# Expert weights of a two-layer diffusion backbone in 1 MB loads of two neighbouring rows, with the slots of SBUF handed out in pairs

## Chip, cores and metric

One core of a Trainium2 chip runs the kernel. The metric is the device time of one execution in microseconds, as the median over runs.

## The reference

Two layers work on 256 latent and 256 context tokens of width 1024, all in fp32. Layer 0 mixes tokens with windowed attention, layer 1 with differential attention. A mixture of experts follows in each layer; latent and context tokens go through it in layer 0, latent ones alone in layer 1. Each token is sent to 2 of 32 experts (the best group of 8, and the two best in it):

```python
u = xblk @ w_up[e]                                      # 1024 -> 1024
y = (silu(u[:, :512]) * u[:, 512:]) @ w_down[e]         # 512 -> 1024
```

The weighted results are added to the tokens. Shift, scale and gate of every part come from `mod_w` (2 x 1024 x 6144) times SiLU of a condition vector. A final RMSNorm gives the output.

## The kernel before

The expert weights are 402.7 MB, 4 MB for one `w_up` and 2 MB for one `w_down`. Every expert is computed, for at most 64 tokens each; a branch (`tc.If`, ahead of the sixth pair) has a slow path for more. A loop runs over 16 pairs of experts per layer. For one pair, `gather` picks tokens with a one-hot matrix, `spread_tokens` turns them so that the model dimension lies on the partitions, `up` multiplies by `w_up` in 8 steps of 128 rows, `gate` makes the gated values, `turned` turns them, `down` multiplies by `w_down` in 4 steps, and `combine` adds the weighted result to the tokens. The last pair uses `down_last`, which goes by four blocks of 256 output columns, so that the end can follow block by block. TensorE's order is written out by hand in these stages, in the output projection of layer 0 and in all of layer 1; elsewhere a scheduler of the framework orders it, and it orders the other engines and the DMA queues throughout.

Most of SBUF is an arena of 43 slots of 512 KB, 128 partitions by 4 KB. `Slot()` takes one from the list `free`, `free()` puts it back at the end. Both act while the program is written, in the order of the code; on the chip, whoever writes a slot waits until its former readers are done.

All weights pass through `plan`, a list of sources in the order of use, and `Stream`. Each entry is one DMA of 512 KB on SP's queue into a slot of its own (`one`, L172 to L178). `next` issues an entry at the place in the code where its weight is used; it can run ahead on the chip as far as its slot has been out of use. Entries are issued further ahead at the start (20 of them) and before the branch (`ahead`).

Attention weights are used in fp32 halves: `split` (L510) takes the raw slot, and two more for a high part (ScalarE copy, L513) and a low part (subtraction on VectorE or GpSimd, L517), and gives the raw one back. The output projection of layer 0 has four rounds of two splits each (L1364), 24 matmuls (L1373) for each of two blocks.

Layer 1 begins in `start1` (L1413): three slots of extra row buffers (`Extra`), one for tables (`Home`), four splits ahead, eight slots `hT` for the normalized tokens, then projections for two halves of v, then k, then q. Each projection takes a split from `ws` for every two of its eight steps and calls `pre` (L1446), which keeps `ws` filled: one raw chunk, split on ScalarE and GpSimd, and then `late_mods` with 0 to 4 chunks of layer 1's `mod_w`. Each such chunk is 256 rows by 512 columns and is multiplied and added up on VectorE (L1507, L1509). There are 32 of them, by `LATE`: 4 in each of four calls, then 3 in each of four, then 1 in each of four, and none in the last eight. `late_sum` (L1476) adds the results over partitions on TensorE, four accumulators at a time.

```python
def late_mods(n):
    ...
        s, w = stream.next()
        for kk in range(2):
            ...
        s.free()
```

Of the kernel before, what the change touches and what calls it, by code (L numbers as in the profile page):

```python
# [56 lines left out]
def _hybrid_dit(ctx, tc, a, out):  # L57
# [5 lines left out]
    places = [[nc.alloc_sbuf_tensor_at(f"slot{c}{i}", [128, 1024], dt, offset=base + 4096 * i).ap()  # L63
               for c, dt in (("f", F32), ("r", F32R))] for i in range(SLOTS)]
    const = ctx.enter_context(tc.tile_pool(name="const", bufs=1))
    pool = ctx.enter_context(tc.tile_pool(name="act", bufs=1))
# [45 lines left out]
    free = list(range(SLOTS))  # L112

    class Slot:
        def __init__(self, recent=False):
            assert free, "no slot left"
            self.s = free.pop(-1 if recent else 0)

# [10 lines left out]
        def free(self):  # L129
            free.append(self.s)  # L130
            self.s = None

    class Ring:
# [29 lines left out]
    class Stream:  # L163
# [23 lines left out]
    def plan_mod(l, third, halves, k):  # L187
        w = a["mod_w"][l, k * 128:(k + 2) * 128]
        for h in halves:
            for q in range(2):  # L190
                c0 = third * 2048 + q * 1024 + h * 512
                plan.append((w[:, c0:c0 + 512].rearrange("(q p) n -> p q n", p=128), (2, 512)))

    def plan_cols(src, c0, ks=range(0, KT, 2)):
        for k in ks:
            plan.append((src[k * 128:(k + 2) * 128, c0:c0 + 512].rearrange("(q p) n -> p q n", p=128), (2, 512)))

    def plan_out(src):
        for n in range(4):
            for k in range(0, KT, 4):  # L200
                plan.append((src[k * 128:(k + 4) * 128, n * 256:(n + 1) * 256].rearrange("(q p) n -> p q n", p=128),
                             (4, 256)))

    def plan_experts(l):
        for p in range(NE // 2):
            for k in range(KT):
                for s in range(2):
                    plan.append((a["moe_w_up"][l, 2 * p + s, k * 128:(k + 1) * 128, :], (1024,)))
            for k in range(4):
                for s in range(2):  # L210
                    w = a["moe_w_down"][l, 2 * p + s]
                    if p + 1 < NE // 2:
                        plan.append((w[k * 128:(k + 1) * 128, :], (1024,)))
                    else:
                        plan.append((w[:, k * 256:(k + 1) * 256].rearrange("(q p) n -> p q n", p=128), (4, 256)))

    late_cols = [(c, h, k) for c in (3, 2, 4, 5) for h in range(2) for k in range(0, KT, 2)]

    def plan_late(n):
        for _ in range(n):  # L220
            c, h, k = late_cols.pop(0)
            c0 = c * 1024 + h * 512
            plan.append((a["mod_w"][1, k * 128:(k + 2) * 128, c0:c0 + 512].rearrange("(q p) n -> p q n", p=128),
                         (2, 512)))

    wq0, wq1 = a["win_w_qkv"][0], a["diff_w_qkv"][0]
    mod_steps = [(m // 3, m % 3, (0, 1), k) for m in range(1, 4) for k in range(0, KT, 2)]
    for d in range(4):
        for k in range(0, KT, 4):
            for q in range(2):  # L230
                c0 = q * 1024 + d * 256
                plan.append((a["mod_w"][0, k * 128:(k + 4) * 128, c0:c0 + 256].rearrange("(q p) n -> p q n", p=128),
                             (4, 256)))
        plan_cols(wq0, 1024, (2 * d,))
# [14 lines left out]
    for k in range(KT):  # L249
        plan.append((a["diff_w_o"][0, k * 128:(k + 1) * 128, :], (1024,)))  # L250
    plan_experts(1)
# [178 lines left out]

    x_slots = [Slot(recent=True) for _ in range(KT // 2)]
    xT = [x_slots[k // 2].f(2, 512)[:, k % 2] for k in range(KT)]
# [400 lines left out]
    v0s.free()  # L833

    def logit_bias(l, nr):
        ps = bank("G")
        for k in range(KT):
# [11 lines left out]
    def part(v, c0, nt, n):  # L849
        return v[:, c0:c0 + nt * n].rearrange("p (t n) -> p t n", t=nt)  # L850

    class Post:
        def __init__(self, l, nt, lb=None):
# [5 lines left out]
            if nr == 2:  # L859
# [3 lines left out]
                for h in range(2):  # L863
                    dg = row("x")
                    for k in range(4):
                        ve.tensor_scalar(dg[:, k * 128:(k + 1) * 128], ident, d[:, 4 * h + k:4 * h + k + 1], None,
                                         op0=OP.mult)
                    ps = bank("G")
                    pe.matmul(ps, ones, dg, start=True, stop=True)
                    se.activation(self.db.f()[:, h * 512:(h + 1) * 512], ps, AF.Copy)  # L870
            self.norm = Norm(self.T, 2 if nr == 2 else 4, ge, tags="s" if nr == 2 else "st")
# [14 lines left out]
        def scaled(self, k):  # L886
            l = self.l
            if k % 4 == 0:
                self.xs[k // 4] = [Slot() for _ in range(2)]
            xa = self.xs[k // 4][k % 4 // 2].f(2, 512)[:, k % 2, :self.T]  # L890
# [16 lines left out]
        def flip(self, h, tags, ks=range(4)):  # L907
            for t in range(self.nt):
# [3 lines left out]
                for k in ks:  # L912
                    pe.transpose(ps[:, k * 128:(k + 1) * 128], self.xa[4 * h + k][:, t * 128:(t + 1) * 128], ident)
                cs = slice(ks[0] * 128, (ks[-1] + 1) * 128)
                hs = slice(h * 512 + ks[0] * 128, h * 512 + (ks[-1] + 1) * 128)
                if t < 2 and len(self.tok[t]) > 1:
                    hi, lo = (v[:, hs] for v in self.tok[t])
                    se.activation(hi, ps[:, cs], AF.Copy)
                    ve.tensor_tensor(lo, ps[:, cs], hi.bitcast(F32), op=OP.subtract)
                elif self.nr == 1:  # L920
                    se.activation(self.slots[t][-1].f()[:, hs], ps[:, cs], AF.Copy, scale=self.ri[:, t:t + 1])
                elif t % 2 == 0:
                    se.activation(self.slots[t][-1].f()[:, hs], ps[:, cs], AF.Copy)
                else:
                    ve.tensor_copy(self.slots[t][-1].f()[:, hs], ps[:, cs])
            if ks[-1] == 3:
# [51 lines left out]
    def moe(l, nt, post, after, finish):  # L978
# [77 lines left out]
        for p in range(np_):  # L1056
# [17 lines left out]
            if p == IF_AT:  # L1074
# [116 lines left out]
    def spread_tokens(l, st, h):  # L1191
        ps = bank("G")
        for k in range(4):
            pe.transpose(ps[:, k * 128:(k + 1) * 128], st["x"][h][:, k * 128:(k + 1) * 128], ident)  # L1194
        o = row("t")
        ve.tensor_tensor(o.rearrange("p (k c) -> p k c", k=4), ps.rearrange("p (k c) -> p k c", k=4),  # L1196
                         mods[l][:, 3, 4 * h:4 * h + 4, 0:1].to_broadcast([128, 4, 128]), op=OP.add)
        st["xt"].append(o)

    def up(st, u, k):  # L1200
        w = [stream.next() for _ in range(2)]
        for h in range(2):
            for s in range(2):
                c0 = (k % 4) * 128 + 64 * s
                pe.matmul(u[h][64 * s:64 * s + 64, :], st["xt"][k // 4][:, c0:c0 + 64],  # L1205
                          w[s][1][:, h * 512:(h + 1) * 512], start=(k == 0), stop=(k == KT - 1))
        for s in range(2):
            w[s][0].free()

    def gate(u):  # L1210
        th, ac = row("s"), row("s")
        se.activation(th, u[0], AF.Tanh, scale=0.5)  # L1212
        ve.scalar_tensor_tensor(ac, th, 1.0, u[0], op0=OP.add, op1=OP.mult)  # L1213
        ve.scalar_tensor_tensor(ac, ac, 0.5, u[1], op0=OP.mult, op1=OP.mult)
        return ac
# [25 lines left out]
    def down(acT):  # L1241
        y = [bank("B"), bank("B")]
        for k in range(4):
            w = [stream.next() for _ in range(2)]
            for h in range(2):
                for s in range(2):
                    c0 = k * 128 + 64 * s
                    pe.matmul(y[h][64 * s:64 * s + 64, :], acT[:, c0:c0 + 64],  # L1248
                              w[s][1][:, h * 512:(h + 1) * 512], start=(k == 0), stop=(k == 3))
            for s in range(2):  # L1250
                w[s][0].free()
        return y
# [41 lines left out]
    def overflow(l, nt, key, W, ri, tok, hT):  # L1294
        T = nt * 128
        for t in range(nt):
            for h in range(2):
# [13 lines left out]
                for k in range(4):  # L1311
                    ve.tensor_scalar(hT[4 * h + k][:, t * 128:(t + 1) * 128], ps[:, k * 128:(k + 1) * 128],
                                     mods[l][:, 3, 4 * h + k, 0:1], None, op0=OP.add)
        Wov = row("p", (128, nt, NE))
# [5 lines left out]
        with tc.For_i(0, NE, 1) as i:  # L1320
# [12 lines left out]
            ve.tensor_copy(wrow[:, :T], ps[:, :T])  # L1333
            wu = a["moe_w_up"][l, bass.ds(i, 1)].rearrange("o (k p) n -> p (o k) n", p=128)
            wd = a["moe_w_down"][l, bass.ds(i, 1)].rearrange("o (k p) n -> p (o k) n", p=128)
# [178 lines left out]
    def move_x(after):  # L1514
        slots = [Slot() for _ in range(2)]
        with tc.issue_after(after.ins):
# [270 lines left out]
```

## Time and profile before

| | us |
|---|---|
| median of three runs (1555.31 to 1561.44) | 1558.62 |
| profiled execution, its own time | 1559.65 |
| its span, first to last instruction | 1557.9 |
| TensorE busy | 1459.4 (94%) |
| VectorE busy | 692.2 (44%) |
| ScalarE busy | 385.2 (25%) |
| GpSimd busy | 186.2 (12%) |

The mean DMA rate is 312 GB/s over 485.67 MB. Busy shares are means over stages with different limits: layer 0's attention ends near 214 us and its output projection near 280, layer 0's experts run to about 815 us, layer 1's attention to about 1052, its experts to the end. DMA time is the time in which a packet was under way on an engine, so it can exceed the stretch by a little.

### The profile page before, as it was taken

Reading aid. Unit: us, or ns where it says so; the run is one execution under the profiler, and the core shown is the slowest. Engines: PE = TensorE matmul, PEld = TensorE weight load, DVE = VectorE, ACT = ScalarE, POOL = GpSimd, SP = SyncE. Lnnn points to the kernel's source line nnn. Section 1 sums busy time; section 2 is a strip of 40 time slices with the busy share of each in tenths; the row PEclk is TensorE's granted clock in tenths of the full one; section 3 lists DMA queues with packets and bytes.
Section 4 is the critical chain, followed back from the end, with each engine's and each line's share of the span. In section 5 each row is a group of like instructions: output and inputs, shape, how many; then the busy total and the mean of one; then the engine's idle time right before and its main releaser. Section 6 shows DMA issues by size and latency. Waiting matters only on the chain. (4 is left out here: it accounts for less than half of the span.)

```text
span 1557.9 us, 20210 instructions
## 1 busy us (share of the span) xinstructions
PE 1459.4 (94%) x7407; PEld 802.0 (51%) x7407; DVE 692.2 (44%) x1617; ACT 385.2 (25%) x823; POOL 186.2 (12%) x147
## 2 busy tenths in 40 slices
PE   6998999799999999999997889798999899999997
PEld 4765567444444454445445578684434343443444
DVE  3348862533333343334348976863223232332333
ACT  4426652211100111001123236552111110110112
POOL 2314541000000000000014364100000000000000
PEclk9999999799999999999997999998999999999999
DMA  9777225799989999999963842477999999999992
GB/s 329 245 230 250 82 96 194 281 373 399 390 348 393 399 398 386 402 399 399 381 210 95 287 168 81 167 272 279 388 409 409 408 409 409 409 409 409 409 396 73
DMA packets 169696, 485.67 MB, mean 312 GB/s; under 512 B 20826, under 2 KB 41587, under 8 KB 169587
## 3 DMA queue, kind: packets, MB, share of 16 engines
q1 hardware_dynamic: 169088, 483.66, 81.9%
q8 instruction: 63, 1.03, 0.3%
q10 hardware_dynamic: 498, 0.60, 0.1%
q14 instruction: 47, 0.38, 0.1%
HBM read 483.16 MB, written 1.05 MB: 311 GB/s over the span
## 5 line engine op out<-in xcount | busy, mean ns | idle before, releaser
L1205 PE MATMUL ps<-slotf,row 128*64 128x512 f32 x2048 | 450.8, 595 | 2.1 <-DVE row L1196 2.1
L1205 PEld LDWEIGHTS ps<-slotf,row 128*64 128x64 f32 x2048 | 145.6, 137 | 291.1 <-issue 275.3
L1248 PE MATMUL ps<-slotf,row 128*64 128x512 f32 x960 | 212.6, 595 | 0.0
L542 PE MATMUL ps<-slotr,slotr 128*128 128x512 f32 x768 | 193.6, 405 | 9.5 <-DVE slotf L1410 4.2
L505 DVE SCALAR_TENSOR_TENSOR slotf<-ps,mod,slotf 128x256 f32<-128x256 f32 x408 | 167.3, 476 | 62.4 <-PE ps L1287 29.7
L542 PEld LDWEIGHTS ps<-slotr,slotr 128*128 128x128 f32 x768 | 145.1, 194 | 48.2 <-DVE slotf L1410 5.0
L1248 PEld LDWEIGHTS ps<-slotf,row 128*64 128x64 f32 x960 | 66.2, 137 | 124.9 <-issue 118.1
L1213 DVE SCALAR_TENSOR_TENSOR row<-row,ps 128x512 f32<-128x512 f32 x30 | 20.6, 688 | 234.4 <-ACT row L1212 234.4
L1212 ACT ACTIVATE row<-ps 128x512 f32<-128x512 f32 x30 | 17.9, 597 | 427.8 <-PE ps L1205 388.4
L1274 DVE SCALAR_TENSOR_TENSOR row<-ps,ty,row 128x512 fp32r<-128x512 f32 x60 | 45.1, 751 | 176.4 <-ACT row L1273 173.2
L1273 ACT ACTIVATE row<-ps,ty 128x512 fp32r<-128x512 f32 x60 | 41.3, 688 | 262.9 <-PE ps L1248 262.6
L1287 PE MATMUL ps<-row,row 128*128 128x512 f32 (+1 forms) x512 | 104.5, 349 | 1.1 <-DVE slotf L505 1.0
L1287 PEld LDWEIGHTS ps<-row,row 128*128 128x128 f32 x512 | 77.3, 189 | 36.6 <-ACT row L1212 21.1
L517 POOL TENSOR_TENSOR slotr<-slotf,slotr 128x1024 fp32r<-128x1024 f32 x32 | 81.0, 2543 | 90.0 <-ACT slotr L513 62.0
L1196 DVE TENSOR_TENSOR row<-ps,mod 128x512 f32<-128x512 f32 x64 | 42.7, 687 | 102.4 <-PE ps L1194 101.7
L477 POOL TENSOR_TENSOR row<-row,row 128x512 f32<-128x512 f32 (+1 forms) x13 | 15.0, 1157 | 576.0 <-PE ps L1287 519.9
L1148 PE MATMUL ps<-slotf,row 128*128 128x512 f32 x128 | 65.3, 634 | 6.9 <-PEq L1081 4.7
L1148 PE MATMUL ps<-slotr,row 128*128 128x512 f32 x256 | 70.6, 420 | 0.0
L513 ACT ACTIVATE slotr<-slotf 128x1024 fp32r<-128x1024 f32 x44 | 46.0, 1056 | 49.3 <-DMA slotf<-in_diff_w_qkv 22.9
L1148 PEld LDWEIGHTS ps<-slotr,row 128*128 128x128 f32 x256 | 48.1, 198 | 10.0 <-issue 0.8
L1509 DVE SCALAR_TENSOR_TENSOR row<-slotf,keep,row 128x512 f32<-128x512 f32 x42 | 50.6, 1222 | 1.1
L1373 PE MATMUL ps<-slotr,slotr 128*128 128x512 f32 x192 | 47.6, 399 | 0.0
(311 smaller groups left out, 1552.2 us busy)
## 6 DMA issues: line engine op xcount, KB each, us to landing
slotf<-in_moe_w_up SPq DMA_DIRECT2D x512, 512.0 KB, 9.5
slotf<-in_moe_w_down SPq DMA_DIRECT2D x256, 512.0 KB, 10.1
slotf<-in_mod_w SPq DMA_DIRECT2D x96, 512.0 KB, 6.0
slotf<-in_diff_w_qkv SPq DMA_DIRECT2D x24, 512.0 KB, 4.4
slotf<-in_win_w_qkv SPq DMA_DIRECT2D x12, 512.0 KB, 5.1
slotf<-in_win_w_o SPq DMA_DIRECT2D x8, 512.0 KB, 4.1
slotf<-in_diff_w_o SPq DMA_DIRECT2D x8, 512.0 KB, 4.4
slotf<-in_x SPq DMA_DIRECT2D x2, 512.0 KB, 4.0
```

Source lines behind the costliest of these rows:

```text
L505: ve.scalar_tensor_tensor(xT[k][:, sl], ps[:, sl], g[:, k, r:r + 1], xT[k][:, sl], op0=OP.mult, op1=OP.add)
L513: se.activation(hv, v, AF.Copy)
L517: (eng or (ge if split_i[0] % 3 == 0 else ve)).tensor_tensor(lv, v, hv.bitcast(F32), op=OP.subtract)
L542: pe.matmul(ps[t], h[:, x, ts], w[y][:, kk, :], start=(k + kk == 0 and n == 0), stop=(k + kk == KT - 1 and n == 2))
L1148: pe.matmul(g, P[:, t, :] if len(tok[t]) > 1 else P[:, t, :].bitcast(F32), v[:, hs], start=(t == 0 and i == 0), stop=(t == nt - 1 and i == ...
L1196: ve.tensor_tensor(o.rearrange("p (k c) -> p k c", k=4), ps.rearrange("p (k c) -> p k c", k=4), mods[l][:, 3, 4 * h:4 * h + 4, 0:1].to_bro ...
L1205: pe.matmul(u[h][64 * s:64 * s + 64, :], st["xt"][k // 4][:, c0:c0 + 64], w[s][1][:, h * 512:(h + 1) * 512], start=(k == 0), stop=(k == KT ...
L1248: pe.matmul(y[h][64 * s:64 * s + 64, :], acT[:, c0:c0 + 64], w[s][1][:, h * 512:(h + 1) * 512], start=(k == 0), stop=(k == 3))
L1274: ve.scalar_tensor_tensor(yl, y[h], wsl, yh.bitcast(F32), op0=OP.mult, op1=OP.subtract)
L1287: pe.matmul(out, part[:, c * 128:(c + 1) * 128], st["PT"][:, :T], start=(i == 0), stop=(i == 1))
L1373: pe.matmul(ps, w[x][:, k % 4, ms], oT0[k][1][:, y, :], start=(k == 0 and i == 0), stop=(k == KT - 1 and i == 2))
L1509: ve.scalar_tensor_tensor(acc, w[:, kk, :], keep[:, k + kk:k + kk + 1], acc, op0=OP.mult, op1=OP.add)
```

## The change

Expert weights come as 1 MB DMAs into two neighbouring slots at once (`Wide`). A partition gets two neighbouring rows of the weight, 8 KB in one piece, where it had one row of 4 KB. Row 8p + k of `w_up` then lies on partition p and is used in step k, so the tokens' 1024 columns are dealt out in that order (`deal`, `dealt` at the evacuations) and the shift that is added to them is turned likewise (`turned_shift`, new, called in `logit_bias`). Row 4p + k of `w_down` asks the same of the gated values (`gate`). The last pair's `w_down` keeps its 512 KB loads.

Slots 2i and 2i + 1 are partners; slot 42 has none. `Wide` takes the pair that has been whole for longest. `Slot()` takes the first slot of the list whose partner is not in the list, and the first of the list if there is none. `buddies` takes a whole pair for two single slots: `x_slots`, the gathered tokens' slots, the scaled copies, and `move_x` use it. All other slots, those of `split`, `hT`, `Extra` and of all loads of 512 KB among them, use `Slot()`.

```diff
+    def whole_pairs():
+        at = {i: n for n, i in enumerate(free)}
+        found = [(max(at[i], at[i + 1]), i) for i in range(0, SLOTS - 1, 2) if i in at and i + 1 in at]
+        return [i for _, i in sorted(found)]
+
     class Slot:
-        def __init__(self, recent=False):
-            assert free, "no slot left"
-            self.s = free.pop(-1 if recent else 0)
+        def __init__(self, recent=False, at=None):
+            if at is None:
+                assert free, "no slot left"
+                order = free[::-1] if recent else free
+                at = next((i for i in order if i ^ 1 not in free), order[0])
+            free.remove(at)
+            self.s = at
...
+    class Wide:
+        def __init__(self):
+            self.at = whole_pairs()[0]
+            free.remove(self.at)
+            free.remove(self.at + 1)
...
         def one(self):
-            src, shape = plan[self.pos]
+            src, shape, wide = plan[self.pos]
             self.pos += 1
-            s = Slot()
+            s = Wide() if wide else Slot()
             v = s.f(*shape)
-            nc.sync.dma_start(v, src)
+            nc.sync.dma_start(wide_places[s.at // 2] if wide else v, src)
...
     def plan_experts(l):
         for p in range(NE // 2):
-            for k in range(KT):
+            for j in range(KT // 2):
                 for s in range(2):
-                    plan.append((a["moe_w_up"][l, 2 * p + s, k * 128:(k + 1) * 128, :], (1024,)))
...
+                    w = a["moe_w_up"][l, 2 * p + s].rearrange("(p k) n -> p (k n)", k=KT)
+                    plan.append((w[:, j * 2048:(j + 1) * 2048], (2, 1024), True))
+            if p + 1 < NE // 2:
+                for j in range(2):
+                    for s in range(2):
+                        w = a["moe_w_down"][l, 2 * p + s].rearrange("(p k) n -> p (k n)", k=4)
+                        plan.append((w[:, j * 2048:(j + 1) * 2048], (2, 1024), True))
...
+    def turned_shift(l):
...
+        pe.transpose(ps[0:8, 0:128], mods[l][:, 3, :, 0], ident)
+        ve.tensor_copy(row8[0:8], ps[0:8, 0:128])
...
+        pe.matmul(ps[:, 0:128], each, row8[0:8], start=True, stop=True)
...
+    def dealt(v, k0, n):
+        return v.rearrange("t (b m) -> t b m", b=8)[:, :, 16 * k0:16 * (k0 + n)]
+
+    def deal(v):
+        return v.rearrange("t (m b) -> t b m", b=8)
...
-            self.slots = [[Slot() for _ in range(1 if t in WHOLE[l] else 2)] for t in range(nt)]
+            if WHOLE[l]:
+                self.slots = [[s] for s in buddies()]
+            else:
+                self.slots = [list(buddies()) for t in range(nt)]
...
-                    se.activation(self.slots[t][-1].f()[:, hs], ps[:, cs], AF.Copy, scale=self.ri[:, t:t + 1])
+                    se.activation(raw, src, AF.Copy, scale=self.ri[:, t:t + 1])
...
-                stream.ahead(len(free) - 1)
+                stream.ahead(len(stream.ready) + len(whole_pairs()))
...
     def up(st, u, k):
-        w = [stream.next() for _ in range(2)]
+        if k % 2 == 0:
+            st["w_up"] = [stream.next() for _ in range(2)]
+        w = st["w_up"]
...
-        ve.scalar_tensor_tensor(ac, ac, 0.5, u[1], op0=OP.mult, op1=OP.mult)
+        ve.scalar_tensor_tensor(ac.rearrange("s (k p) -> s p k", k=4), th.rearrange("s (p k) -> s p k", k=4), 0.5,
+                                u[1].rearrange("s (p k) -> s p k", k=4), op0=OP.mult, op1=OP.mult)
```

## Rows read from the trace of the kernel before

**Rows 1.** Busy time (and instructions) of each engine by stretch, clock, DMA.
```profile
core 0: us, PE busy (x) PEld busy (x) DVE busy (x) ACT busy (x) POOL busy (x), PEclk, DMA share, GB/s
500.00:700.00 200.00, 198.28 (x960) 94.58 (x958) 76.83 (x171) 22.55 (x36) 0.00 (x0) 1.00 1.01 397
842.00:916.00 74.00, 66.51 (x281) 51.60 (x280) 72.31 (x74) 22.41 (x32) 36.13 (x13) 0.98 0.73 256
1300.00:1500.00 200.00, 196.24 (x942) 83.11 (x942) 58.31 (x122) 22.76 (x41) 0.00 (x0) 1.00 1.03 409
```
**Rows 2.** TensorE in order of time (start, length): two neighbouring pairs per layer.
```profile
362.26 7.04 PE L1205 MATMUL ps<-slotf,row 128*64 128x512 f32 x32
...
394.03 7.04 PE L1205 MATMUL ps<-slotf,row 128*64 128x512 f32 x32
...
1299.80 1.88 PE L1148 MATMUL ps<-slotf,row 128*128 128x512 f32 x4
...
1328.99 1.88 PE L1148 MATMUL ps<-slotf,row 128*128 128x512 f32 x4
```
**Rows 3.** All of TensorE's waits, 1100 to 1500 us: total, times, longest.
```profile
PE ps L1194 <- DVE row L1152: 5.8, 13, 0.4
PE ps L1148 <- PEq L1081: 4.7, 1, 4.7
```
**Rows 4.** Lines L1509, L513, L517: min/median/max ns, first and last start.
```profile
L1509 DVE SCALAR_TENSOR_TENSOR row<-slotf,keep,row x42: 739/752/2901, 842.6 to 913.5; 128x512 f32<-128x512 f32 x42
...
L513 ACT ACTIVATE slotr<-slotf x44: 1040/1060/1067, 16.8 to 955.7; 128x1024 fp32r<-128x1024 f32 x44
...
  DMA slotf<-in_diff_w_qkv: 22.9, 12
...
L517 POOL TENSOR_TENSOR slotr<-slotf,slotr x32: 2335/2396/3820, 18.0 to 956.9; 128x1024 fp32r<-128x1024 f32 x32
...
L517 DVE TENSOR_TENSOR slotr<-slotf,slotr x12: 1212/1224/1943, 48.0 to 240.4; 128x1024 fp32r<-128x1024 f32 x12
```
**Rows 5.** Line L921, and who waited for line L840 (us, times).
```profile
L921 ACT ACTIVATE slotf<-ps,ri x4: 680/688/697, 1058.8 to 1060.5; 128x512 f32<-128x512 f32 x4
...
  PEld ps L844: 1.4, 2
  PE ps L844: 0.9, 1
```
**Rows 6.** DMA issues (KB each, median us to landing): 800 to 842 us; whole span.
```profile
slotf<-in_mod_w SPq DMA_DIRECT2D x4, 512.0 KB, 4.1
slotf<-in_diff_w_qkv SPq DMA_DIRECT2D x2, 512.0 KB, 3.6
...
slotf<-in_win_w_o SPq DMA_DIRECT2D x8, 512.0 KB, 4.1
```
**Rows 7.** TensorE in order of time: output projection, first projection, second `late_sum`.
```profile
241.76 5.75 PE L1373 MATMUL ps<-slotr,slotr 128*128 128x512 f32 x24
...
832.16 24.72 PE L542 MATMUL ps<-slotr,slotr 128*128 128x512 f32 x96 [1.66 <-ACT slotr L1439]
...
936.27 1.07 PE L1476 MATMUL ps<-row,ones 128*32 128x512 f32 x8
```
**Rows 8.** SP's queue in order of time, before the second expert stage.
```profile
1015.05 0.33 SPq L177 DMA_DIRECT2D slotf<-in_moe_w_down  x1
1017.40 5.45 SPq L177 DMA_DIRECT2D slotf<-in_moe_w_up  x3
```
**Rows 9.** TensorE in order of time: first and last `down_last` of each layer.
```profile
801.30 3.67 PE L1260 MATMUL ps<-slotf,row 128*64 128x256 f32 x32 [1.28 <-ACT row L1230]
...
809.03 1.95 PE L1260 MATMUL ps<-slotf,row 128*64 128x256 f32 x16
...
1535.10 3.67 PE L1260 MATMUL ps<-slotf,row 128*64 128x256 f32 x32 [1.24 <-ACT row L1230]
...
1543.15 1.95 PE L1260 MATMUL ps<-slotf,row 128*64 128x256 f32 x16
```

More of the change, by code (lines that the diff above doesn't have):

```diff
@@ L64, in _hybrid_dit @@
                for c, dt in (("f", F32), ("r", F32R))] for i in range(SLOTS)]
+    wide_places = [nc.alloc_sbuf_tensor_at(f"slotw{i}", [128, 2048], F32, offset=base + 8192 * i).ap()
+                   for i in range(SLOTS // 2)]
     const = ctx.enter_context(tc.tile_pool(name="const", bufs=1))
@@ L131, in free, with buddies, f @@
             self.s = None
+    def buddies():
+        at = whole_pairs()
+        if not at:
+            return Slot(), Slot()
+        return Slot(at=at[0]), Slot(at=at[0] + 1)
+    class Wide:
[3 more added lines that the diff above has]
+            free.remove(self.at + 1)
+        def f(self, *shape):
+            return wide_places[self.at // 2].rearrange("p (a b) -> p a b", a=shape[0])
+        def free(self):
+            free.extend((self.at, self.at + 1))
     class Ring:
@@ L191, in plan_mod @@
                 c0 = third * 2048 + q * 1024 + h * 512
[L192 removed]
+                plan.append((w[:, c0:c0 + 512].rearrange("(q p) n -> p q n", p=128), (2, 512), False))
     def plan_cols(src, c0, ks=range(0, KT, 2)):
         for k in ks:
[L196 removed]
+            plan.append((src[k * 128:(k + 2) * 128, c0:c0 + 512].rearrange("(q p) n -> p q n", p=128), (2, 512), False))
     def plan_out(src):
@@ L249, in _hybrid_dit @@
     for k in range(KT):
-        plan.append((a["diff_w_o"][0, k * 128:(k + 1) * 128, :], (1024,)))
+        plan.append((a["diff_w_o"][0, k * 128:(k + 1) * 128, :], (1024,), False))
     plan_experts(1)
@@ L429, in mod_run @@
                 done()
-    x_slots = [Slot(recent=True) for _ in range(KT // 2)]
+    x_slots = [s for _ in range(KT // 4) for s in buddies()]
     xT = [x_slots[k // 2].f(2, 512)[:, k % 2] for k in range(KT)]
@@ L833, in _hybrid_dit @@
     v0s.free()
+    moe_shift = {}
+    def turned_shift(l):
+        work = row("x")
+        mod16 = homes[l].v[:, 964:980]
+        ve.tensor_reduce(mod16, ident.rearrange("p (k a) -> p a k", a=16), axis=AX.X, op=OP.add)
+        row8, t = work[:, 0:128], work[:, 128:256].rearrange("p (b a) -> p b a", b=8)
+        ps = bank("G")
+        pe.transpose(ps[0:8, 0:128], mods[l][:, 3, :, 0], ident)
+        ve.tensor_copy(row8[0:8], ps[0:8, 0:128])
+        ps = bank("G")
+        each = work[0:8, 256:384]
+        ve.tensor_copy(each.rearrange("j (k a) -> j k a", k=8), ident[0:8, 0:8].unsqueeze(2).to_broadcast([8, 8, 16]))
+        pe.matmul(ps[:, 0:128], each, row8[0:8], start=True, stop=True)
+        ve.tensor_tensor(t, ps[:, 0:128].rearrange("p (a b) -> p b a", b=8), mod16[:, None, :].to_broadcast([128, 8, 16]),
+                         op=OP.mult)
+        moe_shift[l] = const.tile([128, KT], F32, name=f"shift{l}", tag="shift")
+        ve.tensor_reduce(moe_shift[l], t, axis=AX.X, op=OP.add)
     def logit_bias(l, nr):
+        turned_shift(l)
         ps = bank("G")
@@ L888, in scaled @@
             if k % 4 == 0:
-                self.xs[k // 4] = [Slot() for _ in range(2)]
+                self.xs[k // 4] = buddies()
             xa = self.xs[k // 4][k % 4 // 2].f(2, 512)[:, k % 2, :self.T]
@@ L1205, in up @@
                 pe.matmul(u[h][64 * s:64 * s + 64, :], st["xt"][k // 4][:, c0:c0 + 64],
-                          w[s][1][:, h * 512:(h + 1) * 512], start=(k == 0), stop=(k == KT - 1))
-        for s in range(2):
-            w[s][0].free()
+                          w[s][1][:, k % 2, h * 512:(h + 1) * 512], start=(k == 0), stop=(k == KT - 1))
+        if k % 2:
+            for s in range(2):
+                w[s][0].free()
     def gate(u):
@@ L1243, in down @@
         for k in range(4):
-            w = [stream.next() for _ in range(2)]
+            if k % 2 == 0:
+                w = [stream.next() for _ in range(2)]
             for h in range(2):
@@ L1248, in down @@
                     pe.matmul(y[h][64 * s:64 * s + 64, :], acT[:, c0:c0 + 64],
-                              w[s][1][:, h * 512:(h + 1) * 512], start=(k == 0), stop=(k == 3))
-            for s in range(2):
-                w[s][0].free()
+                              w[s][1][:, k % 2, h * 512:(h + 1) * 512], start=(k == 0), stop=(k == 3))
+            if k % 2:
+                for s in range(2):
+                    w[s][0].free()
         return y
@@ L1514, in move_x @@
     def move_x(after):
-        slots = [Slot() for _ in range(2)]
+        slots = buddies()
         with tc.issue_after(after.ins):
```

44 lines of the change are left out of this document (22 added, 22 removed).

## The prediction

> **What bounds the kernel now.** I read the table of stages first. In both expert stages TensorE is busy 98 to 99% of the time while the DMA engines also look full: 397 GB/s in the first layer, 409 GB/s in the second [rows 1]. Two full resources cannot both set the pace, so the next view is TensorE's order of time. One pair of experts takes 394.03 − 362.26 = 31.77 us in layer 0 and 1328.99 − 1299.80 = 29.19 us in layer 1 [rows 2]. Then its waits: in 400 us of layer 1 it waits 5.8 us for a VectorE copy, 4.7 us for the branch, and never for a weight [rows 3]. So TensorE sets the pace and the loads run ahead of it. At 409 GB/s one pair (12.58 MB) takes 30.76 us to load, longer than 29.19: layer 1 lives on weights fetched earlier, and loses 1.6 us of that lead per pair.
>
> The reader is then to see where loads do matter: outside the expert stages. From 842 to 916 us VectorE is busy 72.31 of 74 us [rows 1], because it adds up the 32 late chunks of `mod_w` (`late_mods`), two operations of 0.75 us for each [rows 4]. The chunks are there in time because each lands in another of some 20 free slots (counted through the code): the list is a queue, and a slot is used again only after all others.
>
> **The change, part by part.** *DMAs.* In the expert stages each layer's 384 issues become about 190, of 1 MB. Nothing waits for them now, so faster pieces are worth 0 there. What hides the loads is the lead; were it gone at the start of layer 1, 16 pairs × (30.76 − 29.19) = 25 us would show. Pairs come whole later than single slots in the attention ahead, so I take 3 of 0 to 25. Against this stands a page of the Trainium skill, "DMA: Bandwidth & Descriptors", section "Rules for kernel authors": use at least 1 MiB per DMA for the best bandwidth. By it the stage would shorten; by [rows 3] there is no wait that it could remove.
>
> *Matmuls* stay the same in number and shape. *Shuffled columns:* the gate's write and some twenty evacuations of token columns get strides. No strided one is in the rows; layer 1's four plain ones take 0.69 us each [rows 5], and the router's VectorE chain runs meanwhile. Between 0 and double, 4 × 0.69 = 2.8 us a layer, I take 1 in all. *`turned_shift`* adds two TensorE operations and some six on VectorE per layer, with one hand-over from TensorE to VectorE and back. The nearest such hand-over, `logit_bias`'s copy, made TensorE wait 0.9 us and its weight load 1.4 us over two layers [rows 5]; 0 to 5, taken as 2.
>
> *The free list.* This is the part I price highest. `Slot()` no longer takes the oldest slot. It takes the oldest whose partner is taken, a loose half; only without one does it break the oldest whole pair. Slot 42 has no partner and is always loose. With exactly one loose half, a stream of single-slot loads gets that same slot again and again: each DMA must wait until the reader of the chunk before is done. I followed the list by hand through the code.
>
> Layer 1's start. After the last expert pair all is whole but 42. `Extra` takes 42 and a pair A, A'. `Home` takes B. Four splits take B', C, C' / D, D', E / E', F, F' / G, G', H (raw, high, low). As raw slots are freed, hT's eight take H', B', D, I, I', E', G and J; J' is left loose. The projection's first two chunks give back the pair C, C' and the halves D' and E. Now `pre` is called for the first time: raw takes J', high D', low E, and J' is free again and the only loose half. All four late chunks take J'. The second call does the same (raw J', a whole pair for high and low, four chunks in J'). Then `v1s` takes J', G', H and breaks a pair, which leaves L'. From there all ten further calls that have late chunks put raw and late chunks into L': when D' and E come back, the next high and low take them again.
>
> The price of one link: a chunk lands 3.6 us after a lone issue (4.1 with four together) [rows 6], VectorE then reads it in 2 × 0.75 us [rows 4], and hand-overs take some 0.3: 5.4 us. A call's raw chunk costs 3.6 + ScalarE's 1.06 + GpSimd's 2.40 [rows 4] + 0.3 = 7.4 us. The Trainium skill bears on this link: the same page, in "Anatomy of one DMA", fits 2.0 us plus bytes over 436 GB/s, an estimate of 3.2 us for 512 KB, and its rules say to issue early and wait late, which one slot forbids. With 3.2 for 3.6 the 32 chunks would cost 13 us less; the rows' 3.6 is used.
>
> J' starts when the second chunk's matmuls end: the four chunks take 24.72 us from 832.16 [rows 7], so at 844.5. Its split's 3.5, four links (21.6), 7.4 and four links bring it to 898.6. L' carries 10 × 7.4 + 24 × 5.4 = 204 us. If it runs beside J' from 845 on, the sums are ready at 1049; if SP's queue, which is in order, keeps it behind J', at 1103. SP's order is not the plan's: of an expert's loads, `w_down` go out among `w_up` [rows 8], so a load whose slot is free overtakes. That row is nearer to the first case; I take 1060. Who waits: the matmuls of the second `late_sum` stand in TensorE's fixed order. They now run at 936.27 [rows 7], 22 us after VectorE's last late operation (913.5 + 0.75) [rows 4]. Add 5 us for the query chunks that come ahead of them: 1065 − 936 = **129 us later**, ends 115 and 172.
>
> *Tails.* In each layer the last pair's four steps of `down_last` load two single slots each, and 42 is again the only loose half: step c + 1's first DMA waits for step c's matmuls. Such a load lands in 4.1 us (`win_w_o`, the same shape) [rows 6], with 0.4 of hand-over and 1.95 of matmuls [rows 9]: 6.45 a step, 3 × 6.45 + 1.95 = 21.3 us. Now the four take 810.98 − 801.30 = 9.7 and 1545.10 − 1535.10 = 10.0 us [rows 9]. Cost 11.6 + 11.3 = **23 us**. Behind the first tail's DMAs on SP wait layer 1's tables and first `diff_w_qkv` chunks; the norm ahead of 832 covers them. Without that cover 4 us more.
>
> *Layer 0's output projection.* The loose halves are 11, 14 and 41 (partners hold `oT0`). Of the two splits in each of four rounds both take raw 11. The second's DMA waits for the first's subtraction: 4.1 + 1.06 + 1.22 (VectorE) to 2.40 (GpSimd) = 6.4 to 7.6 us [rows 4, 6], against the first half of the block's 24 matmuls, 2.9 us [rows 7]: about 4 a round, **16 us**, ends 0 (splits run ahead) and 30. *Layer 0's queries:* every second chunk's high half takes the previous chunk's low slot, four times 2.3 to 3.5 us, but TensorE's order is free there: 6, ends 0 and 26 (with 4.1 for the modulation load behind each).
>
> Sum: 129 + 23 + 16 + 6 + 3 + 2 + 1 = 180 us, on the profiled execution's 1559.65 us (its span is 1557.9; the median of the runs is 1558.62, 1 us less): **1740 us**. With all low ends it is 1559.65 + 115 + 23 = 1698; with all high ends 172 + 27 + 30 + 26 + 25 + 5 + 6 = 291 more, 1850.
>
> **Rivals.**
> *Enough halves go round (not slower).* Before, 32 chunks take 74 us, 2.3 us each. If three or more loose halves went round in layer 1, a link would cost 5.4 / 3 = 1.8 us, under 2.3, and the tails' loads would also be early: from three halves on nothing is lost and the time is 1559.65 + 3 + 2 + 1 = 1566, or 1563 with the lead whole, within the bound below. For it: some 20 slots are free at that time. Against it: they are whole pairs, and the hand count gives one. Chance 7%.
> *Larger pieces shorten the stage.* TensorE's waits for weights would be its gain, and they are 0 in [rows 3]. What is left are the loads behind the expert weights: ScalarE waited 22.9 us in all for `diff_w_qkv` [rows 4]. If sooner expert loads halved that and TensorE gained all of it, with no chain, the time were 1559.65 − 11 = 1549. Chance 3%.
> *Only part of the chain is on the path.* If a second half came loose before the second projection, the 204 us of L' would halve: sums at 845 + 102 = 947 to 899 + 102 = 1001, with the 5 us 16 to 70 us late; with the tails' 23 that gives 1599 to 1653. Against it: D' and E come back only to be taken by the next call. Chance 8%.
> *Layer 1's lead is lost as well* and SP keeps the order: 1850 and over. Chance 6%.
> The forecast, one slot for each chain, has 76%.
>
> **Numbers.** Predicted 1740. The forecast's case runs from 1698 to 1850, its bounds, and holds 76%; taking in the upper half of the partial case, 1625 to 1850 holds 8 in 10. What a measurement of this kernel can tell from no change is 0.5%, 7.8 us. Faster: 4%, the larger-pieces case and a little of the first. Same: 6%, the rest of the first. Slower: 90%.
>
> **What would show it.** After 845 us: VectorE idle before `late_mods`' operations for `mod_w` loads, 4 us each, its busy share there falling from 98% to under half; SP waiting for VectorE or GpSimd before each load; the second `late_sum` 100 to 170 us later than the end of layer 0 would put it. In the tails TensorE idle 4 us before each step for a `w_down` load. In the output projection three or four gaps of some 4 us. The pairs' 31.77 and 29.19 us unchanged, with no waits for weights. Wrong would be the prediction if the late chunks land in different slots (VectorE stays full), if a link is well under 5 us, or if the expert stages' periods move.

## The result, and the profile after

The changed kernel takes **1773.27 us** (median of four runs, 1773.09 to 1779.74) against 1559.33 (1555.31 to 1561.44) for the kernel before on the same chip: a ratio of 1.139, 95% interval 1.135 to 1.142. It is slower, as forecast; 1740 was 33 us short, and the time lies in the range of 1625 to 1850. The profiled execution has a span of 1771.7 us where before had 1557.9, so 213.8 us are to be found. Six points in TensorE's order of time place them:

| start or end on TensorE (us) | before | after | later in this stretch | forecast |
|---|---|---|---|---|
| first `up` of layer 0 | 299.61 | 322.82 | 23.2 | 22 (queries 6, output projection 16) |
| end of the last `up` of layer 0 | 797.52 | 824.88 | 4.2 | 0 (1 in all for strides) |
| second `late_sum` | 936.27 | 1128.53 | 164.9 | 129, and 11.6 for the tail ahead of it |
| first `up` of layer 1 | 1069.85 | 1267.05 | 4.9 | 2 (`turned_shift`) |
| end of the last `up` of layer 1 | 1531.32 | 1726.89 | -1.6 | 3 (lead) |
| end of the span | 1557.9 | 1771.7 | 18.2 | 11.3 (tail) |

In the third stretch 15.7 us lie before the sums that open layer 1's norm, which start at 815.49 before and 858.53 after; 149.2 lie behind them.

The page's 40 slices show the hole at once. A slice is 44 us; the digits of TensorE, VectorE and the granted clock fall together in slices 20 to 26, from about 840 to 1150 us, and the DMA engines are less than half busy there, so it is not bandwidth that is short:
```profile
PE   6999987899999999998633533788899989999996
...
DVE  3247743333333334343532221587332323232322
...
PEclk9999999899999999999676865899999999999995
DMA  9567036699899999994143323144899999999951
GB/s 338 172 214 274 2 126 234 267 401 400 332 399 401 380 401 396 385 400 132 40 142 95 107 83 107 48 179 151 338 391 422 400 419 421 421 421 422 420 224 60
```
The table of stages gives the sizes. Before, VectorE was busy 98% of the stretch with the late chunks [rows 1]. Now it is at 22.19 and 29.68 of 100 us there, and the second expert stage is unharmed:
```profile
core 0: us, PE busy (x) PEld busy (x) DVE busy (x) ACT busy (x) POOL busy (x), PEclk, DMA share, GB/s
...
930.00:1030.00 100.00, 43.39 (x147) 31.53 (x148) 22.19 (x32) 10.47 (x17) 14.26 (x6) 0.69 0.34 100
1030.00:1130.00 100.00, 42.06 (x125) 28.58 (x123) 29.68 (x40) 15.32 (x19) 27.36 (x13) 0.65 0.31 94
...
1290.00:1500.00 210.00, 201.84 (x965) 85.98 (x965) 62.18 (x126) 23.33 (x42) 0.00 (x0) 0.99 0.99 410
```
VectorE in order of time shows the chain link by link (start, length, and in brackets the idle time before and what ended it; L1577 and L1579 are `late_mods`):
```profile
929.04 1.54 DVE L1579 SCALAR_TENSOR_TENSOR row<-slotf,keep,row 128x512 f32<-128x512 f32 x2 [3.77 <-DMA slotf<-in_mod_w]
934.34 1.54 DVE L1579 SCALAR_TENSOR_TENSOR row<-slotf,keep,row 128x512 f32<-128x512 f32 x2 [3.77 <-DMA slotf<-in_mod_w]
939.64 1.54 DVE L1579 SCALAR_TENSOR_TENSOR row<-slotf,keep,row 128x512 f32<-128x512 f32 x2 [3.75 <-DMA slotf<-in_mod_w]
...
952.04 0.49 DVE L1577 TENSOR_SCALAR slotf<-slotf,keep 128x512 f32<-128x512 f32 x1 [10.27 <-DMA slotf<-in_mod_w]
```
From one late chunk to the next it is 5.30 us: 1.54 of work and 3.77 in which VectorE waits for a load that was only issued once VectorE had finished with the half (issued at 930.61, the work that began at 929.04 having ended at 930.58). From 939.64 to 952.04 it is 12.4, a raw chunk and a late one. SP's waits in the same stretch (860 to 1130; total, times, longest) name what the loads wait for: the landing of the load before, and its readers, a splitting subtraction on GpSimd (L551) and the late operations:
```profile
SPq L206 <- POOL slotr L551: 100.5, 14, 41.4
SPq L206 <- DMA slotf<-in_mod_w: 61.2, 25, 4.2
SPq L206 <- DVE row L1579: 33.4, 21, 3.7
```
And TensorE's waits (820 to 1130) show who waits at the end: the projection (L576) for split chunks, `late_sum` (L1546) for the last accumulator, and `down_last` (L1330) for its loads:
```profile
PE ps L576 <- ACT slotr L547: 66.8, 7, 16.2
PE ps L576 <- DVE slotf L1480: 38.4, 2, 36.9
PE ps L1546 <- DVE slotf L1579: 17.1, 1, 17.1
PE ps L576 <- POOL slotr L551: 12.0, 7, 2.3
PE ps L1330 <- DMA slotf<-in_moe_w_down: 10.1, 3, 4.5
```

### The profile page after: what moved, and what is told of

The parts are those of the page before. It is cut to its first block, busy times and chain, and to the rows that moved or that the text cites. A ratio compares the mean times of both kernels' runs of the same rounds, so it can differ in the third digit from the quotient of the medians.

```text
span 1771.7 us, 19500 instructions
## 1 busy us (share of the span) xinstructions
PE 1508.5 (85%) x7413; PEld 826.1 (47%) x7413; DVE 686.2 (39%) x1627; ACT 386.5 (22%) x823; POOL 179.3 (10%) x147
## 5 line engine op out<-in xcount | busy, mean ns | idle before, releaser
L1271 PE MATMUL ps<-slotw,row 128*64 128x512 f32 x2048 | 449.2, 593 | 2.1 <-DVE row L1260 2.1
L576 PE MATMUL ps<-slotr,slotr 128*128 128x512 f32 x768 | 218.8, 438 | 129.0 <-ACT slotr L547 67.2
L1271 PEld LDWEIGHTS ps<-slotw,row 128*64 128x64 f32 x2048 | 144.9, 137 | 290.2 <-issue 281.8
L576 PEld LDWEIGHTS ps<-slotr,slotr 128*128 128x128 f32 x768 | 157.7, 212 | 181.5 <-ACT slotr L547 71.9
L1317 PE MATMUL ps<-slotw,row 128*64 128x512 f32 x960 | 212.6, 595 | 0.0
L1317 PEld LDWEIGHTS ps<-slotw,row 128*64 128x64 f32 x960 | 66.1, 137 | 125.0 <-issue 125.0
L551 POOL TENSOR_TENSOR slotr<-slotf,slotr 128x1024 fp32r<-128x1024 f32 x32 | 75.9, 2378 | 266.0 <-ACT slotr L547 256.2
L1260 DVE TENSOR_TENSOR row<-ps,shift 128x512 f32<-128x512 f32 x64 | 42.7, 686 | 101.3 <-PE ps L1258 100.5
L1579 DVE SCALAR_TENSOR_TENSOR row<-slotf,keep,row 128x512 f32<-128x512 f32 x42 | 36.9, 877 | 92.3 <-DMA slotf<-in_mod_w 91.5
L1443 PE MATMUL ps<-slotr,slotr 128*128 128x512 f32 x192 | 50.9, 413 | 8.0 <-ACT slotr L547 3.8
```

The source lines that it names most:

```text
L551: (eng or (ge if split_i[0] % 3 == 0 else ve)).tensor_tensor(lv, v, hv.bitcast(F32), op=OP.subtract)
L576: pe.matmul(ps[t], h[:, x, ts], w[y][:, kk, :], start=(k + kk == 0 and n == 0), stop=(k + kk == KT - 1 and n == 2))
L1317: pe.matmul(y[h][64 * s:64 * s + 64, :], acT[:, c0:c0 + 64], w[s][1][:, k % 2, h * 512:(h + 1) * 512], start=(k == 0), stop=(k == 3))
L1443: pe.matmul(ps, w[x][:, k % 4, ms], oT0[k][1][:, y, :], start=(k == 0 and i == 0), stop=(k == KT - 1 and i == 2))
```

## The experiments

Two theories stood against each other. *The rule*: a lone free half is taken again and again, so a load waits for the reader of the load before it; each of the lead, the chain and the tails is a place where that happens. *The loads*: 1 MB transfers, or their need of whole pairs, cost the time, and the half only names who waits. The kernels start from the changed one, e5 and e6 from e1.

**e1, no preference for lone halves.**
```diff
-                at = next((i for i in order if i ^ 1 not in free), order[0])
+                at = order[0]
```


> The changed kernel, but Slot() always takes the slot that has been free longest, as before the change; the 1 MB loads, their pairs of slots, the column order and turned_shift stay. Theory (a lone free half is taken again and again, so that a load waits for the use of the load before it): the 213.8 us by which the profiled span grew go, apart from what the other parts cost, which the two traces put at 30 gates x 0.39 us = 12 and about 2 for turned_shift: 1573 us (1560 to 1585). Rival (the 1 MB loads or their need of whole pairs cost the time, and the rule only names who waits): still above 1700.

Measured: 1567.35 us, 1.0046 of before (1.0032 to 1.0060). One line gives back 206 of 214 us with every 1 MB load still in place. In layer 1's attention VectorE waits for no late chunk any more, and the second `late_sum` comes 140.3 us behind the end of layer 0's last `up` (138.8 before, 303.7 after). The rival is excluded. That `late_sum` in TensorE's order of time, first in the changed kernel and then in e1:
```profile
1128.53 1.94 PE L1546 MATMUL ps<-row,ones 128*32 128x512 f32 x8
...
942.94 1.06 PE L1546 MATMUL ps<-row,ones 128*32 128x512 f32 x8
```

**e2, 1 MB as two loads of 512 KB.**
```diff
-            nc.sync.dma_start(wide_places[s.at // 2] if wide else v, src)
+            if wide:
+                for i in range(2):
+                    nc.sync.dma_start(wide_places[s.at // 2][:, i * 1024:(i + 1) * 1024], src[:, i * 1024:(i + 1) * 1024])
+            else:
+                nc.sync.dma_start(v, src)
```


> The changed kernel with its slot rule, but each 1 MB load is issued as two loads of 512 KB (pieces of 4 KB) into the same pair of slots. Theory (the rule, not the size of the loads): 1773 us within 10, with the same idle stretch of TensorE from 860 to 1130. Rival (the size of the loads sets the time): the time moves by more than 40, down towards 1559 if large loads are what hurts, up if they hide part of the loss.

Measured: 1773.40 us, 1.1375 (1.1352 to 1.1398), the time of the changed kernel. Layer 1's pairs take 459.92 us from the first `up` to the end of the last, against 459.84 with 1 MB loads. So the size of the loads, the part that gives the change its name, moves nothing that stands out of the spread of these runs (1766 to 1777). The Trainium skill ("DMA: Bandwidth & Descriptors", "Rules for kernel authors") asks for 1 MiB or more per DMA for the best bandwidth. The page's slices of layer 1's experts do show a higher rate, 421 GB/s in the changed kernel against 409 in e2, but no TensorE wait that it could shorten.

**e3, layer 1's raw and late chunks take the oldest slot.** A flag around `stream.next()` in `late_mods` and around the split in `pre`:
```diff
-                at = next((i for i in order if i ^ 1 not in free), order[0])
+                at = order[0] if oldest[0] else next((i for i in order if i ^ 1 not in free), order[0])
...
+                oldest[0] = True
                 with tc.issue_after(h_made[0].ins):
                     s = split(*stream.next(), (2, 512), ge)
+                oldest[0] = False
...
+            oldest[0] = True
...
             s, w = stream.next()
+            oldest[0] = False
```


> The changed kernel, but the loads and splits that pre issues in layer 1's attention and the chunks of late_mods take the slot free longest; every other Slot() keeps the new rule. Theory (each term stands alone): the 149 us between the end of layer 0's experts and the last late_sum go, the rest stays: 1773 - 149 = 1624 (1610 to 1645). Rival 1 (VectorE's or ScalarE's order in that stage, not the slot, is what it waits for): above 1700. Rival 2 (the load order is given back later, in a next wait of the same stage): 1650 to 1700.

Measured: 1626.03 us, 1.0418 (1.0401 to 1.0436): 147 us come back, both rivals fall.

**e4, the tails' loads take the oldest slot**: the same flag for loads of `moe_w_down`.

> The changed kernel, but the down weights of the last pair of each layer (the eight 512 KB loads of down_last) take the slots free longest; every other Slot() keeps the new rule. Theory: the two tails, 15.7 and 18.2 us later in the trace of after, come back: 1773 - 34 = 1739 (1733 to 1750). Rival (the tails are late for the lower granted clock or for the order of the queue, and the half only names the wait): 1760 to 1775.

Measured: 1743.49 us, 1.1169 (1.1148 to 1.1189): 30 us. The steps of `down_last` show more than the sum. In the changed kernel the last tail reads (TensorE in order of time)
```profile
1730.69 1.95 PE L1330 MATMUL ps<-slotf,row 128*64 128x256 f32 x16 [1.25 <-DVE slotf L539]
1736.23 3.68 PE L1330 MATMUL ps<-slotf,row 128*64 128x256 f32 x16 [3.60 <-DMA slotf<-in_moe_w_down]
...
1743.53 3.68 PE L1330 MATMUL ps<-slotf,row 128*64 128x256 f32 x16 [2.46 <-DMA slotf<-in_moe_w_down]
...
1750.97 3.68 PE L1330 MATMUL ps<-slotf,row 128*64 128x256 f32 x16 [0.26 <-DMA slotf<-in_moe_w_down]
```
and in e4
```profile
1719.48 3.67 PE L1333 MATMUL ps<-slotf,row 128*64 128x256 f32 x32 [1.25 <-DVE slotf L542]
1723.75 1.95 PE L1333 MATMUL ps<-slotf,row 128*64 128x256 f32 x16
1727.53 1.95 PE L1333 MATMUL ps<-slotf,row 128*64 128x256 f32 x16
```
The three waits for loads are 6.3 us in all. The same 16 matmuls take 3.68 us instead of 1.95 behind them; the table of stages puts the granted clock there at 0.50, the 1.2 GHz level, and it stays there up to the end of the span. Before, the matmuls of this stretch ran at 1.00:
```profile
1690.00:1727.00 37.00, 36.46 (x175) 14.67 (x172) 8.74 (x18) 3.99 (x8) 0.00 (x0) 1.00 0.49 189
1727.00:1736.00 9.00, 4.38 (x36) 3.46 (x36) 4.81 (x13) 1.13 (x3) 0.00 (x0) 0.97 0.18 58
1736.00:1752.00 16.00, 13.05 (x58) 8.66 (x60) 2.63 (x6) 4.43 (x10) 0.00 (x0) 0.50 0.21 66
```
So in this execution waits of 6.3 us cost 18.2. The clock's part is not the same in every execution. In the profiled one of e2, with the same rule for slots and the same loads in the tail, the waits are 8.0 us, and the tail is only 11 us longer than before (37.6 against 26.6 from the end of the last `up`), since the clock came back before the last step:
```profile
1735.75 3.24 PE L1334 MATMUL ps<-slotf,row 128*64 128x256 f32 x16 [3.47 <-DMA slotf<-in_moe_w_down]
...
1742.55 3.26 PE L1334 MATMUL ps<-slotf,row 128*64 128x256 f32 x16 [2.89 <-DMA slotf<-in_moe_w_down]
...
1749.35 1.95 PE L1334 MATMUL ps<-slotf,row 128*64 128x256 f32 x16 [1.64 <-DMA slotf<-in_moe_w_down]
```
Over the traces of e2, e3, e8, e9 and e10, which all keep this tail, it costs 11 to 18 us.

**e8, the lead takes the oldest slot**: the flag is set from the start to the first expert load.

> The changed kernel, but up to the first expert load (layer 0's modulation, queries, attention and output projection) Slot() takes the slot free longest; from there on the new rule. Theory (the 23 us by which layer 0's experts start late are that stage's own loose halves): 1773 - 23 = 1750 (1745 to 1757). Rival (turned_shift and the strided token copies make the start late): 1765 to 1775.

Measured: 1748.63 us, 1.1219 (1.1198 to 1.1240); the first `up` is at 298.77. The lead is the rule's, too. With e3 and e4 the three pieces give back 147 + 30 + 25 = 202 of the 206 us of e1: the terms add up.

**e9 and e10, one of the two streams alone.** e9 sets the flag in `late_mods` only, e10 in `pre` only.

> The changed kernel, but only the chunks of late_mods take the slot free longest; the raw chunks and their splits in layer 1's attention keep the new rule, and most raw chunks then follow one another in one half. Theory (the stage is long because raw and late chunks take turns in one half, four late links of 5.3 and a raw one of 7.4 for each chunk of the projection; a raw chain by itself has a link of 7.4 against 6.2 us of TensorE's own work for a chunk, 24.72 / 4): 16 chunks x 1.2 = 19 above the 1626 of e3: 1645 (1630 to 1660). Rival 1 (the raw chunks hold the larger part): above 1690. Rival 2 (the late chunks alone): 1626 within 5.

> The changed kernel, but only the raw chunks that pre loads in layer 1's attention and their splits take the slot free longest; the late chunks keep the new rule, and find three or four lone halves in rotation, since whole pairs are now opened. Theory (one half in rotation is what costs, whoever waits in it): as with three halves in e7, where this stage was 27 longer than in e1: 1626 + 27 = 1653 (1635 to 1670). Rival (the late chunks alone make the chain of 5.3 a link): above 1720.

Measured: 1640.52 (1.0520, 1.0502 to 1.0537) and 1630.24 us (1.0452, 1.0433 to 1.0471). Freeing either stream is nearly as good as freeing both (1626.03), but the two runs do not say the same. Followed through the code, e9 leaves ten raw chunks in a row in one half: a raw chain by itself costs about 14 us. e10 leaves no chain at all: the raw chunks and their splits open whole pairs, the 32 late chunks fall into 18 slots, and a slot is taken again by the third load after it at the soonest, mostly later. Its forecast of three or four halves was wrong, which fits a time 5 us below its range. So what a chain of late chunks alone would cost was not tried; as an estimate, 32 links of 5.30 are 170 us, where all 32 chunks took 74 before [rows 1]. e9 also isolates the raw link. ScalarE's splits (L548) follow each other in one half:
```profile
927.79 1.06 ACT L548 ACTIVATE slotr<-slotf 128x1024 fp32r<-128x1024 f32 x1 [8.24 <-DMA slotf<-in_diff_w_qkv]
935.20 1.06 ACT L548 ACTIVATE slotr<-slotf 128x1024 fp32r<-128x1024 f32 x1 [5.87 <-DMA slotf<-in_diff_w_qkv]
942.76 1.06 ACT L548 ACTIVATE slotr<-slotf 128x1024 fp32r<-128x1024 f32 x1 [3.08 <-DMA slotf<-in_diff_w_qkv]
950.30 1.06 ACT L548 ACTIVATE slotr<-slotf 128x1024 fp32r<-128x1024 f32 x1 [6.48 <-DMA slotf<-in_diff_w_qkv]
```
935.20 - 927.79 = 7.4 us, then 7.6 and 7.5; but one link of 7.5 per chunk is close to the 24.72 / 4 = 6.2 us [rows 7] that TensorE needs for it, and so almost hidden.

**e7, three halves go round.**
```diff
-                at = next((i for i in order if i ^ 1 not in free), order[0])
+                loose = [i for i in order if i ^ 1 not in free]
+                at = loose[0] if len(loose) >= 3 else order[0]
```


> The changed kernel, but Slot() prefers a lone free half only while at least three are free, and takes the slot free longest otherwise; in layer 1's attention the raw and the late chunks then go round three halves in place of one. Theory (a chunk waits for the use of the chunk that had its half before, 5.3 us a link with one half): with three halves a third of that, 1.8 us a link, which the stage's own work nearly hides: 1570 to 1590. Rival (any preference for lone halves costs: 149 us divided by three stays, beside the lead of 23): about 1640.

Measured: 1611.87 us, 1.0329 (1.0313 to 1.0345), between both: a miss for the theory's number. Against e1 the first `up` is 11.6 us later, the second `late_sum` another 27.4 and layer 1's first `up` another 5.9. VectorE's waits (850 to 1000) name the loads again:
```profile
DVE row L1580 <- DMA slotf<-in_mod_w: 20.3, 11, 5.0
...
DVE row L1578 <- DMA slotf<-in_mod_w: 7.5, 3, 3.1
DVE slotf L1578 <- DMA slotf<-in_mod_w: 6.3, 2, 3.7
```
The estimate of 1.8 us a link took the three halves for the late chunks alone. Followed through the code, the three do go round, but the raw chunks take their turn in them as well: (32 x 5.3 + 12 x 7.4) / 3 = 86 us where the stretch took 74 before [rows 1], which makes 12 of the 27 us, as an estimate. SP waits 39.5 us for the late operations and 36.6 for GpSimd's subtraction in this stretch; what the rest of the 27 us is made of was not tried.

**e5 and e6, the gate's strided write.** What is left in e1 is mostly in layer 0's pairs, 4.9 us longer than before. e5 writes the gated values in plain order and so leaves out their turn to the order of the `w_down` rows; e6 puts it back by letting the transposes of `turned` read every fourth column. (The second part of the diff is e6's alone.)
```diff
-        ve.scalar_tensor_tensor(ac.rearrange("s (k p) -> s p k", k=4), th.rearrange("s (p k) -> s p k", k=4), 0.5,
-                                u[1].rearrange("s (p k) -> s p k", k=4), op0=OP.mult, op1=OP.mult)
+        ve.scalar_tensor_tensor(ac, th, 0.5, u[1], op0=OP.mult, op1=OP.mult)
...
-            pe.transpose(ps[:, k * 128:(k + 1) * 128], ac[:, k * 128:(k + 1) * 128], ident)
+            pe.transpose(ps[:, k * 128:(k + 1) * 128], ac.rearrange("s (p k) -> s k p", k=4)[:, k], ident)
```


> e1_oldest (1567.35 us) with the second operation of gate() writing in the plain order again, 0.68 us where the strided one takes 1.06; the gated values then have not the order of the down rows, which this kernel leaves out. Theory (the strided write is late for gather in layer 0 only: there TensorE's wait for VectorE's copies at the end of gather doubles, 1.7 to 3.4 us in 6 pairs): the layer-0 pairs come back by 5 us, layer 1 is unchanged: 1562.5 (1560 to 1565). Rival 1 (the gate is on the path in both layers, 30 x 0.39): 1556. Rival 2 (it is hidden, and the 1 MB loads make the pairs longer): 1567.

> e5_gate_plain, with the column order of the gated values made in turned(): its four transposes read every fourth column of the plain tile, and nothing of the computation is left out. Theory (TensorE reads 128 columns at a stride of 4 as fast as neighbouring ones, 0.27 us each): the time of e5 within 2, about 1562.5, no faster than the kernel before within 0.3%. Rival (a strided read slows the transposes): e5 plus 120 x what each takes longer.

Measured: 1564.50 (1.0027, 1.0016 to 1.0038) and 1564.43 us (1.0028, 1.0017 to 1.0039). Layer 0's pairs come back by 3.7 and 4.2 us, layer 1's do not move. The strided operation of e1 (line L1281, least, median, longest in ns) and TensorE's wait behind it (300 to 800 us; the transposes of `gather`, L1228, wait for small VectorE copies, L1253, that come after the gate's write) are
```profile
L1281 DVE SCALAR_TENSOR_TENSOR row<-row,ps x30: 1034/1072/1101, 318.9 to 1510.2; 128x512 f32<-128x512 f32 x30
...
PE ps L1228 <- DVE ty L1253: 7.4, 13, 0.6
```
and in e6 that wait is
```profile
PE ps L1228 <- DVE ty L1253: 3.6, 13, 0.3
```
The plain form takes 0.68 us, and the wait was 3.7 before. In e6 a strided transpose takes 0.283 us where the plain one takes 0.273, and its weight load 0.209 for 0.140; nobody waits for it. e6 does all that the change set out to do and is still 0.3% above the kernel before: no version with 1 MB loads was found that beats it. What these last 0.3% are made of was not tried.

## Why the prediction held, point by point

The sum was 33 us short: 20 in the late chain, 11 in the tails, the rest in small terms of both signs.

**Nothing to gain in the pairs.** Held, and e2 shows it from the other side. Layer 1's pairs, priced 3 us longer for the lead, came out 1.6 shorter; layer 0's grew for another reason (see strided columns).

**The hand count of halves.** Held: one half for each chain. A link of 5.4 us measured 5.30, and the raw chunk's 7.4 measured 7.4 to 7.6 (e9). The rows' landing time was the better choice: VectorE's idle 3.77 contains the landing, at a median of 3.7 in that stretch. The fit in the Trainium skill ("DMA: Bandwidth & Descriptors", "Anatomy of one DMA"), an estimate of 3.2 us for such a load, is one for DMAs that GpSimd issues, and these go out on SP's queue.

**The late chain, 129, measured 149: how far the two chains overlap was mis-sized.** Of the two cases "beside J'" (sums at 1049) and "behind it" (1103), 1060 was taken, near the first. The last late operation ends at 1126.2; without the 43.0 us by which the stage starts later (858.53 - 815.49) that is 1083, between the two. VectorE's order shows operations on two accumulators, one `row` and one `slotf`, alternating from 892 to 913, four chunks of each chain, and one chain alone from 924. J' kept to the count: its last chunk is read at 941.2, or 898.2 without the 43.0, where 898.6 was forecast. L' did its first four chunks beside it and then stood still until 944.84, when ScalarE could split its next raw chunk; ScalarE had waited for TensorE, and TensorE 36.9 us for a copy of a finished v tile (L1480). The copy comes right behind J's last late operation (939.64 + 1.54):
```profile
941.09 0.68 DVE L1480 COPY slotf<-ps 128x512 f32<-128x512 f32 x1
```
By the hand count that fits: the first slot of `v1s` is J' itself, and the v tile can go there only when the last chunk in it has been read. The prediction has this slot in its count, but no wait for it. That the slot, and not VectorE's order alone, held the copy back was not tried by itself. Part of the wait was put in the wrong place as well: the forecast named only `late_sum` as the waiting matmuls, but TensorE lost more in the projection, 66.8 us for ScalarE's splits and 38.4 for the copies. `late_sum` itself waited 17.1. (Two small slips hardly change the forecast: the low end of 115 is 118 by its own numbers, 1049 + 5 - 936, and the last late operation before ended at 916.4 and not 914.3.)

**The tails, 23, measured 33.9: mis-sized.** The waits were shorter than forecast (10.1 us in the first tail, 6.3 in the second). The term priced the matmuls at their old 1.95 us and left out the clock: they took 2.97 to 3.68, and what follows the last of them is slowed as well. In e2's second tail, where the clock came back, the cost is 11 us, the forecast's 11.3. That the half is the cause of both, waits and clock, is shown by the 30 us of e4.

**The lead, 22, measured 23.2: the sum is right, its two parts are less sure.** The queries and what follows them were priced at 6, the output projection at 16, about 4 a round. Counted from the projection's first matmul, which still stands among the attention's (213.99 before, 222.44 after), the parts are 8.4 and 14.3, near the forecast; counted from the block of its whole rounds (226.49, 240.69) they are 14.2 and 8.6. The projection's waits for splits, none before, are 8.0 us in all, in gaps of 0.5 to 1.7 and not of some 4:
```profile
253.96 0.73 PE L1443 MATMUL ps<-slotr,slotr 128*128 128x512 f32 x2 [1.74 <-ACT slotr L547]
255.22 2.55 PE L1443 MATMUL ps<-slotr,slotr 128*128 128x512 f32 x10 [0.53 <-DVE slotr L551]
```
So the splits ran ahead further than assumed, within the ends of 0 and 30, and that the sum came out so near is in part luck.

**Strided columns, 1: wrong in kind.** Twenty evacuations were looked at and the gate's write was put with them. It runs 30 times and takes 0.39 us more each time. In layer 0, where `gather` waits for VectorE's small copies behind it, part of it reaches TensorE: about 4 us, the pair going from 31.77 [rows 2] to 32.09.

**Rivals.** That three halves would make the loss vanish was ruled out here by the count, but e7 shows that its condition was wrong as well: with three in rotation 45 us of e1's gain are gone. Followed through the code, no second half came loose for L'. Larger pieces did not shorten a stage, and layer 1's lead was not lost.

## What to carry to other kernels

A free list decides on the distance between a load and the reader that it must wait for: whoever takes the slot freed last turns a prefetch into a round trip. Before an allocator is changed to keep large blocks whole, follow it by hand through the stage with the most single loads, and count how many buffers are really in rotation; link time over that count, and not the sum of free memory, is the least that the stage will pay (e7 paid more). In this case taking the oldest slot kept enough pairs whole for every 1 MB load, so the preference that cost 206 us was not needed. And price a new wait of TensorE with the clock behind it: in the last tail here, waits of 6 to 8 us cost 11 to 18.

## What was not expected of the hardware

Waits of 0.3 to 3.6 us between short matmuls, 6.3 in all, were enough to leave TensorE at a granted clock of 0.50 for the last 35 us of the span, after 0.97 to 1.00 up to then. In e2 waits of 3.47, 2.89 and 1.64 in the same place let it come back to 1.00 by the last step (1749.75 to 1756.75). In layer 0's tail, with waits of 3.71, 4.46 and 1.92, it fell to 0.68 and 0.74. In the long hole TensorE works at 0.65 to 0.73.

A VectorE operation over 128x512 with one operand in PSUM takes 1.07 us when neighbouring elements are written 128 columns apart, 0.68 in the plain order; TensorE's transposes that read every fourth column lose 0.01 us, and their weight loads 0.07.
